# All three branch products of a hybrid mixer by token tile, with the second tile's inputs asked for at that tile

## The chip, the cores and the metric

One core of a Trainium2 chip runs the whole program in one launch. The metric is the device time of one execution in microseconds. Engines: PE multiplies matrices, DVE (vector) and ACT (scalar) work on tiles, POOL does a few small operations, SP issues nearly all transfers. Each engine, and SP's queue too, works through its own instructions in order and waits where one is not ready.

## The reference, cut to what matters

Two layers, each of three blocks on `h` (256 tokens by 1024 channels, float32): a gated feed-forward block, a mixer, a second feed-forward block, each with RMS norms before and after. The mixer projects the normed `h` into the inputs of three branches and three gates:

```python
q, k, v, z, xbc, dt_raw, u, vg, gate_raw = jnp.split(xn @ w_in, split_at, axis=-1)
y_a = moba_attention(q, k, v)                      # 8 heads x 128, causal, ALiBi; 256 tokens are one block
y_s = rms_norm(ssd_scan(...) * jax.nn.silu(z), g)  # state space branch, chunks of 128 tokens
y_c = u * (tril(sgu_w) @ layer_norm(gelu(vg)))     # spatial gating, chunks of 128 tokens
merged = gates[0] * (y_a @ p_attn) + gates[1] * (y_s @ p_ssm) + gates[2] * (y_c @ p_sgu)
return merged @ w_out
```

Tokens lie in two tiles of 128. Attention is causal and the scan runs forward, so the first tile's rows of `y_a` and `y_s` depend on the first tile alone, and the second tile's on both.

## The kernel before, in words

**Matmuls.** Every weight comes as blocks of 128x1024 (512 KB) on SP's queue into a ring of six (`raw`, `load`, L157). `split` (L174) turns a block into two halves, `whi` by a cast on ACT (L180) and `wlo` by a subtraction on DVE (L181), in a ring of `SPLIT` = 11 pairs; splitting a block frees its `raw` buffer and so lets SP issue the next load. `gemm` (L217) walks over (block, token tile): one such **unit** is two products of three matmuls each (L213 to L215: high by high, high by low, low by high; 128x512 each). Activations are held in the same two halves (`xh`, `xl`).

**Order of a gemm.** By default each block is used for tile 0 and then tile 1. The first `head` and the last `tail` blocks go by tile instead: all of them for tile 0, then all of them for tile 1. A block is given back (`done`, L185) at its last unit; only then may another block be split into its place.

**Order of the rest.** All other work is written as generators (`spawn`, L115). After each unit `pump` (L198) advances a counted clock by 1.3 and gives each task its turn when the time that it has yielded has run out; a task's `yield W[...]` is thus a distance counted in units of matmul work. `finish` (L135) runs tasks to their end on the spot. This fixes the order of instructions in each engine's queue; on the chip each engine then runs its queue as the data allow. `pump` also splits at most one waiting block per unit.

**The mixer** (L488, order from L947). Projections `xbc`, `z`, `q`, `k`, `v`; the state space task `ssd` (L678) runs beside `q`, `k` and `v`. For each tile and each group of eight heads it makes decay weights (`ssw`: DVE L709, four exponentials on ACT L713, DVE L715), waits `W["w2"]`, and multiplies (`yd`, L738; for tile 1 also `yo`, L744). At a tile's end it spawns `turned` (L663), which takes `y` through DRAM to turn it (`turn`, L276: a DVE transposition and four DMAs out; `land`, L284: one DMA back) and makes the halves `ysh`, `ysl` (L673 to L675).

`attention` (L781) is one task for both tiles. Per tile: scores (`qk`, L798), bias (L802) and maximum (L807) on DVE, exponentials on ACT (L814), division and `turn` of the probabilities `sc` (L820, L823), `land` (L827), a wait `W["pv"]`, then the products with `v` (`pv`, L837) and their halves `yah`, `yal` (`halves`, L300) in two groups of heads. Tile 1 does not begin before the flag `free` is set, after the first branch.

`branch` (L925) projects one gate (16 units), finishes what its input needs, and multiplies the input with the branch's weights (eight blocks, 16 units, tile `br`); `merge` (L906) multiplies by the gate and adds into `merged`. The first branch is the state space one (with `merged` taken from the ring of 16 large buffers, `b4`), then `vg` is projected, the second is attention's, then `u` is projected, the third is the spatial gating's. The third has `tail=8`, that is, all of its blocks go by tile; the other two have `tail=0`.

Of the kernel before, what the change touches and what calls it, by code (L numbers as in the profile page):

```python
# [12 lines left out]
AF = mybir.ActivationFunctionType  # L13
# [3 lines left out]
P = 128  # L17
# [34 lines left out]
def trunk(ctx, tc, a):  # L52
# [31 lines left out]
    def tr(name):  # L84
        return psum.tile([P, 512], F32, name=name, tag="tr", bufs=TR)

    def small(name, n, dt=F32, bufs=2):
        return sm.tile([P, n], dt, name=name, tag=name, bufs=bufs)
# [161 lines left out]
    def chunk(key, kt=KD, n=512):  # L250
        per = 1024 // n
        return [[(b * per + j, j * n, n, key, b * per + j == 0, b * per + j == kt - 1) for j in range(per)]
                for b in range(kt // per)]
# [22 lines left out]
    def turn(src, m, e=128):  # L276
        V.transpose(src, src)
        rd = dram.tile([m, 4, 32, 4, e], F32, name=f"turn{m}_{e}", tag=f"turn{m}_{e}", bufs=8)
        for b in range(4):
            nc.sync.dma_start(rd[:, :, :, b, :].rearrange("m c i e -> i (m c) e"),  # L280
                              src[32 * b:32 * b + 32].rearrange("p (x e) -> p x e", e=e))
        return rd

    def land(dst, rd):  # L284
        nc.sync.dma_start(dst, rd.rearrange("m c i a e -> (c i) m (a e)"))
# [14 lines left out]
    def halves(ps, hi, lo):  # L300

        p3 = ps.rearrange("p (k t) -> p k t", k=4)
        A.copy(hi, p3)
        V.tensor_tensor(lo, p3, hi.bitcast(F32), op=ALU.subtract)
# [183 lines left out]
    def mixer(l, x, r2, nxt):  # L488
# [189 lines left out]
        def ssd(ysx, rs):  # L678
# [40 lines left out]
            for t in range(NT):  # L719
                for g in range(SG):  # L720
                    weights(t, 2 * g)
                    if t == 0:
                        scaled(g)
                    yield W["w1"]
                    weights(t, 2 * g + 1)
                    if t == 0:

                        pst = tr("state")
                        T.matmul(pst, bc["b"][:, g * P:(g + 1) * P], xw[:, 512 * g:512 * g + 512],
                                 start=True, stop=True)  # L730
                        A.copy(state[:, 512 * g:512 * g + 512], pst)
                    yield W["w2"]
                    c = slice(512 * g, 512 * g + 512)
                    py = tr("yd")
                    for q in (2 * g, 2 * g + 1):
                        for j in range(4):
                            hh = q * 4 + j
                            T.matmul(py[:, (hh - 8 * g) * SP:(hh - 8 * g + 1) * SP], ws[t, q][:, j, :],  # L738
                                     xdt[t][:, hh * SP:(hh + 1) * SP], start=True, stop=True)
                        ws.pop((t, q))  # L740
                    V.tensor_tensor(y[t][:, c], py, y[t][:, c], op=ALU.add)
                    if t == 1:
                        po = tr("yo")
                        T.matmul(po, cT(g, 1), state[:, c], start=True, stop=True)  # L744
                        tmp = b2("yo")
                        V.tensor_tensor(h3(tmp, 8), h3(po, 8),
                                        st["eac"][:, 8 * g:8 * g + 8, None].to_broadcast([P, 8, SP]), op=ALU.mult)
                        V.tensor_tensor(y[t][:, c], y[t][:, c], tmp, op=ALU.add)
                    V.tensor_tensor(y[t][:, c], y[t][:, c], zs[t][:, c], op=ALU.mult)
                rs[t] = rsqrt([sumsq(y[t], "sy")], "rs", 1.0 / D)  # L750
                yt[t] = spawn(turned(t, y[t], pl[:, G_SSM:G_SSM + 8]), wait=1.3 if t else 6.5)
# [26 lines left out]
                A.activation(vv[t][:, 512 * c:512 * c + 512], ps[t], AF.Copy, scale=r2[t])  # L778
            yield W["vv"]

        def attention(yax, free):  # L781
            for t in range(NT):
                while t and not free:
                    yield 0

                m = t + 1
                n = m * P
                per = 512 // n
                sc, s4 = {}, {}
                mx = small("mx", NH)  # L790
                for g in range(2):
                    sc[g] = (b4 if t else b2)("sc", (P, 4 * n))
                    s4[g] = sc[g].rearrange("p (b h j) -> p h b j", h=4, j=32)
                    for u in range(0, 4, per):
                        ps = tr("qk")
                        for j in range(per):
                            hh = u + j
                            T.matmul(ps[:, j * n:(j + 1) * n], qk["q", g][:, hh, t * P:(t + 1) * P],  # L798
                                     qk["k", g][:, hh, 0:n // 32], start=True, stop=True)
                        for j in range(per):  # L800
                            hh = u + j
                            V.scalar_tensor_tensor(s4[g][:, hh], alibi[t].rearrange("p (b j) -> p b j", j=32),  # L802
                                                   2.0 ** -(4 * g + hh + 1),
                                                   ps[:, j * n:(j + 1) * n].rearrange("p (b j) -> p b j", j=32),
                                                   op0=ALU.mult, op1=ALU.add)
                        yield W["qs"]
                    V.tensor_reduce(mx[:, 4 * g:4 * g + 4], s4[g], axis=AX.XY, op=ALU.max)  # L807
                nmx = small("nmx", NH)
                V.tensor_scalar(nmx, mx, -1.0, None, op0=ALU.mult)
                den = small("den", NH)  # L810
                for g in range(2):
                    for j in range(4):
                        c = slice(4 * g + j, 4 * g + j + 1)
                        A.activation(s4[g][:, j], s4[g][:, j], AF.Exp, bias=nmx[:, c], accum_out=den[:, c])  # L814
                    yield W["ex"]
                rden = small("rden", NH)
                V.reciprocal(rden, den)
                rd = {}
                for g in range(2):
                    V.tensor_tensor(sc[g].rearrange("p (b h j) -> p b h j", h=4, j=32),  # L820
                                    sc[g].rearrange("p (b h j) -> p b h j", h=4, j=32),
                                    rden[:, None, 4 * g:4 * g + 4, None].to_broadcast([P, 4 * m, 4, 32]), op=ALU.mult)
                    rd[g] = turn(sc[g], m)  # L823
                    yield 1.3
                yield W["so"]
                for g in range(2):
                    land(sc[g].rearrange("p (m e) -> p m e", m=m), rd[g])  # L827
                yield W["pv"]
                hi, lo = yax.new(t)
                for g in range(2):  # L830

                    pts = sc[g].rearrange("p (m a h j) -> p m h a j", m=m, a=4, h=4)
                    po = tr("pv")
                    for j in range(4):
                        hh = 4 * g + j
                        for k in range(t + 1):
                            T.matmul(po[:, j * P:(j + 1) * P], vv[k][:, hh * HD:(hh + 1) * HD], pts[:, k, j],  # L837
                                     start=k == 0, stop=k == t)
                    halves(po, hi[:, 4 * g:4 * g + 4, :], lo[:, 4 * g:4 * g + 4, :])
                    yield 1.3  # L840


        uu, vg = {}, {}
# [78 lines left out]
                yield W["mg"]  # L922
                yield from to_parts(merged[t], *then.new(t))

        def branch(bx, rs, need, first=False, then=None):  # L925
            store = {}
            es = []
            for c in range(2):
                [ps] = project("gate")
                es.append(spawn(gate_evac(store, c, ps, rs)))  # L930
            finish(*need)
            finish(*es)
            slots, dst = accs("br")
            ready, out = set(), {}

            def on_done(key, t):
                ready.add((key, t))
                if t not in out:
                    out[t] = spawn(merge(t, slots, ready, store, first, then))

            gemm(chunk(0) + chunk(1), bx.h, bx.l, dst, tail=8 if then is not None else 0, on_done=on_done)
            return out

        ysx, yax, ycx, mx = XT("ys"), XT("ya"), XT("yc"), XT("mg")
# [17 lines left out]
        finish(ss)  # L962
        finish(*at)
        free = []
        att = spawn(attention(yax, free))
        b0 = branch(ysx, rs, [ss, *yt.values()], first=True)
        free.append(True)
        gl = []
        for c in range(2):
            gl.append(spawn(gelu_evac(vg, "vg", c, project("vg")[0])))  # L970
        b1 = branch(yax, None, [att, *b0.values()])
        gw = spawn(spatial_weights(l))
        finish(*gl)
        gl = [spawn(gelu_evac(uu, "u", 0, project("u")[0]))]
# [204 lines left out]
```

## Time and profile before

| | us |
|---|---|
| median of three runs | 1488.76 (1488.53 to 1488.9) |
| the profiled execution | 1487.31 |
| its span, first to last instruction | 1485.5 |
| PE busy in it | 1458.3 |
| DVE busy | 970.1 |
| ACT busy | 767.6 |
| mean granted clock of PE | 0.997 of full speed |

Times in the rows are microseconds from the span's start. Layer 0's mixer is used for the stretches; layer 1's runs the same way some 734 us later. In a timeline a row in brackets gives the idle time of that engine just before the instruction and what ended it. The granted clock is a share of full speed: 1.00 is 2.4 GHz, 0.50 is 1.2 GHz.

### The profile page before, as it was taken

How to read it: one execution, taken by the hardware profiler on the slowest of the kernel's cores; microseconds unless marked ns; L12 is line 12 of the kernel's file. 1: busy time of each engine (PE TensorE's matmuls, PEld its weight loads, DVE VectorE, ACT ScalarE, POOL GpSimd, SP SyncE). 2: the span in 40 equal slices, each digit the busy share in tenths (PEclk: the TensorE clock that was granted, in tenths of full speed). 3: DMA queues.
4: the chain of work that ended last, by engine and by line, in shares of the span. 5: the costliest groups of instructions: out<-in, count | busy, mean ns of one | idle time of the engine just before them, and what ended most of it. 6: DMA issues, size and time to landing. Idle time of an engine off the chain costs nothing.

```text
span 1485.5 us, 18564 instructions
## 1 busy us (share of the span) xinstructions
PE 1458.3 (98%) x6706; PEld 1204.4 (81%) x6706; DVE 970.1 (65%) x1188; ACT 767.6 (52%) x1051; POOL 57.0 (4%) x98
## 2 busy tenths in 40 slices
PE   9999999999989999999999999999999899999998
PEld 6888888777878888888888888888778788888886
DVE  6766477777666857666486564876776667676652
ACT  6544367555464537544364443765553644464441
POOL 0000021000000001000000000210000000000000
PEclk9999999999999999999999999999999999999999
DMA  8977655577567445877458874656774765477860
GB/s 291 333 227 255 198 185 183 156 201 246 190 216 228 167 155 197 284 242 255 154 193 281 252 254 128 217 169 172 250 230 155 232 206 170 136 265 245 260 200 28
DMA packets 151003, 312.23 MB, mean 210 GB/s; under 512 B 35456, under 2 KB 76544, under 8 KB 150912
## 3 DMA queue, kind: packets, MB, share of 16 engines
q1 hardware_dynamic: 150336, 310.73, 64.6%
q8 instruction: 52, 0.85, 0.2%
q10 hardware_dynamic: 576, 0.33, 0.1%
q14 instruction: 39, 0.32, 0.1%
HBM read 288.98 MB, written 22.02 MB: 209 GB/s over the span
## 4 chain that ended last, share of the span: by engine, by line
PE 61%; DVE 9%; ACT 3%; DMA 3%; issue 2%; POOL 0%; SPq 0%; DVEq 0%; ACTq 0%; POOLq 0%
PE gu L213 8%; PE gu L215 8%; PE gu L214 8%; DVE wlo L181 5%; PE dn L213 4%; PE dn L215 4%; PE dn L214 4%; PE br L213 3%; PE br L215 3%; PE br L214 3%; ACT whi L180 1%; PE wo L213 1%; PE wo L215 1%; PE u L215 1%; PE u L214 1%
## 5 line engine op out<-in xcount | busy, mean ns | idle before, releaser
L181 DVE TENSOR_TENSOR wlo<-raw,whi 128x1024 fp32r<-128x1024 f32 x495 | 595.3, 1225 | 330.1 <-ACT whi L180 329.5
L180 ACT CAST whi<-raw 128x1024 fp32r<-128x1024 f32 x495 | 512.3, 1051 | 404.5 <-PE gu L215 162.8
L213 PE MATMUL gu<-whi,xh 128*128 128x512 f32 x704 | 276.0, 392 | 1.9 <-ACT xh L328 1.5
L214 PE MATMUL gu<-wlo,xh 128*128 128x512 f32 x704 | 274.9, 390 | 0.0
L215 PE MATMUL gu<-whi,xl 128*128 128x512 f32 x704 | 274.6, 390 | 0.0
L213 PEld LDWEIGHTS gu<-whi,xh 128*128 128x128 f32 x704 | 132.5, 188 | 30.2 <-ACT xh L328 2.0
L215 PEld LDWEIGHTS gu<-whi,xl 128*128 128x128 f32 x704 | 132.5, 188 | 28.2 <-DVE xl L329 0.6
L214 PEld LDWEIGHTS gu<-wlo,xh 128*128 128x128 f32 x704 | 132.5, 188 | 28.2 <-DVE wlo L169 0.9
L213 PE MATMUL dn<-whi,hTh 128*128 128x512 f32 x352 | 137.5, 391 | 0.0
L215 PE MATMUL dn<-whi,hTl 128*128 128x512 f32 x352 | 137.0, 389 | 0.0
L214 PE MATMUL dn<-wlo,hTh 128*128 128x512 f32 x352 | 136.9, 389 | 0.0
L215 PEld LDWEIGHTS dn<-whi,hTl 128*128 128x128 f32 x352 | 66.1, 188 | 13.9
L214 PEld LDWEIGHTS dn<-wlo,hTh 128*128 128x128 f32 x352 | 66.1, 188 | 13.5
L213 PEld LDWEIGHTS dn<-whi,hTh 128*128 128x128 f32 x352 | 66.1, 188 | 13.3
L213 PE MATMUL gate<-whi,xh 128*128 128x512 f32 x192 | 76.6, 399 | 0.0
L215 PE MATMUL gate<-whi,xl 128*128 128x512 f32 x192 | 74.9, 390 | 0.0
L214 PE MATMUL gate<-wlo,xh 128*128 128x512 f32 x192 | 74.8, 389 | 0.0
L328 ACT CAST xh<-xg 128x512 fp32r<-128x512 f32 (+1 forms) x25 | 15.1, 603 | 62.1 <-DVE xg L326 62.1
L713 ACT ACTIVATE ssw<-ssw,nacs 128x128 f32<-128x128 f32 x64 | 20.5, 390 | 49.6 <-DVE ssw L709 49.6
L215 PEld LDWEIGHTS gate<-whi,xl 128*128 128x128 f32 x192 | 36.0, 188 | 7.7
L214 PEld LDWEIGHTS gate<-wlo,xh 128*128 128x128 f32 x192 | 36.1, 188 | 6.9
L417 ACT ACTIVATE silu<-gu,r 128x512 f32<-128x512 f32 (+1 forms) x48 | 31.4, 654 | 19.9 <-PE gu L215 16.2
(239 smaller groups left out, 2229.3 us busy)
## 6 DMA issues: line engine op xcount, KB each, us to landing
raw<-in_mix SPq DMA_DIRECT2D x232, 512.0 KB, 4.4
raw<-in_gu SPq DMA_DIRECT2D x175, 512.0 KB, 4.9
raw<-in_dn SPq DMA_DIRECT2D x88, 512.0 KB, 4.5
turn<-hh SPq DMA_DIRECT2D x160, 64.0 KB, 1.8
hh<-turn SPq DMA_DIRECT2D x40, 256.0 KB, 5.3
row_ffn_post_g<-in_ffn_post_g SPq DMA_DIRECT2D x4, 512.0 KB, 5.2
turnw<-qtok SPq DMA_DIRECT2D x32, 64.0 KB, 2.6
qT<-turnw SPq DMA_DIRECT2D x4, 512.0 KB, 6.1
```

The lines of the kernel that those rows point to most:

```text
L180: A.copy(hi, w)
L181: V.tensor_tensor(lo, w, hi.bitcast(F32), op=ALU.subtract)
L213: T.matmul(o, xh(k, t), hi[:, off:off + n], start=first, stop=False)
L214: T.matmul(o, xh(k, t), lo[:, off:off + n], start=False, stop=False)
L215: T.matmul(o, xl(k, t), hi[:, off:off + n], start=False, stop=last)
L328: A.copy(o_h, xg)
L417: A.activation(silu[t][:, :w], gate(t), AF.Silu, scale=r2[t])
L713: A.activation(w[:, j, :], w[:, j, :], AF.Exp, bias=st["nacs"][:, c:c + 1])
```

## The change

All branch products go by token tile (`tail=8` in every branch). The first two branches no longer finish both tiles' inputs ahead of their gemm: the second tile's input is asked for (`late`, through `guarded` and `gate_on`, which call `finish` at the first use of tile 1) when the order comes to that tile. For that attention becomes one task per tile; the first is finished after the first branch, before `free` is set. Two steps are longer for the second tile: the one ahead of `yd` by 1.3, the one ahead of `pv` by 6.5 of the planner's count.

```diff
@@ ssd
-                    yield W["w2"]
+                    yield W["w2"] + 1.3 * t
@@ attention: the loop over t becomes an argument, its body is moved out by one level and otherwise the same, but for
-        def attention(yax, free):
-            for t in range(NT):
-                while t and not free:
-                    yield 0
+        def attention(t, yax, free):
+            while t and not free:
+                yield 0
...
-                yield W["pv"]
+            yield W["pv"] + 6.5 * t
@@ branch
-        def branch(bx, rs, need, first=False, then=None):
+        def branch(bx, rs, need, late=None, first=False, then=None):
...
-            gemm(chunk(0) + chunk(1), bx.h, bx.l, dst, tail=8 if then is not None else 0, on_done=on_done)
+            if late is not None:
+                bx = guarded(bx, gate_on(late, finish))
+            gemm(chunk(0) + chunk(1), bx.h, bx.l, dst, tail=8, on_done=on_done)
@@ mixer
-        att = spawn(attention(yax, free))
-        b0 = branch(ysx, rs, [ss, *yt.values()], first=True)
+        att = {t: spawn(attention(t, yax, free)) for t in range(NT)}
+        b0 = branch(ysx, rs, [ss], yt, first=True)
+        finish(att[0])
         free.append(True)
...
-        b1 = branch(yax, None, [att, *b0.values()])
+        b1 = branch(yax, None, [*b0.values()], att)
```

## Rows read from the trace of the kernel before

**Rows 1.** The page, its first part: busy time, share of the span and instructions of each engine.

```profile
PE 1458.3 (98%) x6706; PEld 1204.4 (81%) x6706; DVE 970.1 (65%) x1188; ACT 767.6 (52%) x1051; POOL 57.0 (4%) x98
```

**Rows 2.** The waits of PE over the whole span, longest in total first: engine, tile and line, what it waited for, us in total, times, longest.

```profile
PE pv L837 <- DMA sc<-turn: 8.3, 2, 4.2
PE yd L738 <- DVE ssw L715: 4.7, 4, 1.4
PE br L213 <- ACT ysh L674: 3.1, 2, 1.6
...
```

**Rows 3.** The timeline of PE around the second tile's `pv`, layer 0 and then layer 1: start, duration, instruction, count, idle time before it.

```profile
428.28 3.50 PE L837 MATMUL pv<-sc,v 128*128 128x128 f32 x16 [4.09 <-DMA sc<-turn]
431.54 0.48 PE L213 MATMUL gate<-whi,xh 128*128 128x512 f32 x1
...
433.01 1.95 PE L837 MATMUL pv<-sc,v 128*128 128x128 f32 x16
434.71 0.48 PE L213 MATMUL gate<-whi,xh 128*128 128x512 f32 x1
...
1162.30 3.43 PE L837 MATMUL pv<-sc,v 128*128 128x128 f32 x16 [4.16 <-DMA sc<-turn]
```

**Rows 4.** Stretches of the span: from and to, length, busy time of PE, PE's weight loads, DVE, ACT and POOL, then the granted clock of PE, the DMA share and GB/s. The first is the stretch behind the second tile's `pv` wait, the second the one behind the `br` wait.

```profile
428.28:431.50 3.22, 3.22 (x15) 3.22 (x16) 1.82 (x4) 2.46 (x5) 0.00 (x0) 0.52 1.03 388
...
368.00:372.00 4.00, 4.00 (x17) 3.00 (x18) 3.05 (x5) 2.81 (x4) 0.00 (x0) 1.00 0.97 372
```

**Rows 5.** The timeline of PE around `yd`, layer 0: the second group of the first tile, then the two groups of the second tile, each with the instruction that follows it.

```profile
301.04 1.89 PE L738 MATMUL yd<-xs,ssw 128*128 128x64 f32 x16
302.74 0.48 PE L707 MATMUL seg<-acsr,sel 128*128 128x512 f32 x1
...
314.19 1.00 PE L738 MATMUL yd<-xs,ssw 128*128 128x64 f32 x8
...
317.58 1.08 PE L744 MATMUL yo<-state,conv 128*128 128x512 f32 x2
...
330.60 1.00 PE L738 MATMUL yd<-xs,ssw 128*128 128x64 f32 x8
...
333.44 1.08 PE L744 MATMUL yo<-state,conv 128*128 128x512 f32 x2
```

**Rows 6.** The timeline of PE, layer 0: the first tile's first scores; then in the first branch the end of the first unit, the wait for the second tile's halves, the start of the third unit and the first tile's `pv`, behind the fourth unit.

```profile
342.57 1.05 PE L798 MATMUL qk<-kT,qT 128*128 128x128 f32 x8
...
365.95 0.39 PE L215 MATMUL br<-whi,ysl 128*128 128x512 f32 x1
367.88 0.50 PE L213 MATMUL br<-whi,ysh 128*128 128x512 f32 x1 [1.55 <-ACT ysh L674]
...
369.64 0.39 PE L213 MATMUL br<-whi,ysh 128*128 128x512 f32 x1
...
372.37 1.05 PE L837 MATMUL pv<-sc,v 128*128 128x128 f32 x8
```

**Rows 7.** The tile `br`, the instructions that write it: here the second branch's first matmuls, with shortest, median and longest duration in ns, and the first and the last start (layer 0 and layer 1).

```profile
L213 PE MATMUL br<-whi,yah x64: 389/389/389, 447.1 to 1202.1; 128*128 128x512 f32 x64
```

**Rows 8.** The timeline of SP's queue, layer 0: issues of DMAs, merged where one line issues several in a row; the duration of a merged row reaches to the last issue's end. `raw<-in_mix` are weight loads, `turn<-sc` and `sc<-turn` the probabilities' way out and back (first tile, then second), `y<-turn` the second tile's landing of `y`.

```profile
353.80 0.38 SPq L285 DMA_DIRECT2D y<-turn  x1
359.53 0.33 SPq L160 DMA_DIRECT2D raw<-in_mix  x1
361.11 3.73 SPq L280 DMA_DIRECT2D turn<-sc  x8
...
365.91 0.89 SPq L285 DMA_DIRECT2D sc<-turn  x2
...
417.96 5.54 SPq L160 DMA_DIRECT2D raw<-in_mix  x2
423.61 0.93 SPq L285 DMA_DIRECT2D sc<-turn  x2
```

**Rows 9.** DMA issues, KB each and median us from issue to landing: `y<-turn` over the whole span, then `sc<-turn` in the stretch from 364 to 380.

```profile
y<-turn SPq DMA_DIRECT2D x4, 512.0 KB, 5.1
...
sc<-turn SPq DMA_DIRECT2D x2, 256.0 KB, 5.2
```

**Rows 10.** The timeline of DVE, layer 0: the end of the first tile's `ysl` and the first tile's first scores; the second tile's `y` and three splits behind it; `merged` in the first branch; the second tile's first scores.

```profile
349.15 0.69 DVE L675 TENSOR_TENSOR ysl<-y,ysh 128x512 fp32r<-128x512 f32 x1 [0.69 <-ACT ysh L674]
349.76 0.48 DVE L802 SCALAR_TENSOR_TENSOR sc<-con,qk 128x128 f32<-128x128 f32 x2
...
366.49 0.69 DVE L673 TENSOR_TENSOR y<-y,par 128x512 f32<-128x512 f32 x1
...
370.81 3.50 DVE L181 TENSOR_TENSOR wlo<-raw,whi 128x1024 fp32r<-128x1024 f32 x3 [0.27 <-ACT whi L180]
...
389.15 1.29 DVE L916 TENSOR_TENSOR merged<-br,gate 128x512 f32<-128x512 f32 x2 [9.46 <-PE br L214]
...
397.22 0.41 DVE L802 SCALAR_TENSOR_TENSOR sc<-con,qk 128x256 f32<-128x256 f32 x1
```

**Rows 11.** The stretch of the third branch's product, layer 0, columns as in rows 4.

```profile
518.10:541.00 22.90, 22.90 (x108) 18.93 (x107) 14.36 (x18) 10.91 (x14) 0.00 (x0) 1.00 0.44 142
```

**Rows 12.** The line of `pv`, looked at around the first tile's products: the semaphore instructions of PE's weight load queue, with the first and the last time, in layer 0 and in layer 1.

```profile
L837 PEldq EVENT_SEMAPHORE  x2: 51/51/51, 371.0 to 371.9; - x2
...
L837 PEldq EVENT_SEMAPHORE  x2: 51/51/51, 1105.1 to 1105.8; - x2
```

More of the change, by code (lines that the diff above doesn't have):

```diff
@@ L779, in v_evac @@
             yield W["vv"]
-        def attention(yax, free):
-            for t in range(NT):
-                while t and not free:
-                    yield 0
[L786 to L827, printed above, removed]
-                yield W["pv"]
[L829 to L840, printed above, removed]
@@ new lines, in attention @@
+        def attention(t, yax, free):
+            while t and not free:
+                yield 0
+            m = t + 1
+            n = m * P
+            per = 512 // n
+            sc, s4 = {}, {}
+            mx = small("mx", NH)
+            for g in range(2):
+                sc[g] = (b4 if t else b2)("sc", (P, 4 * n))
+                s4[g] = sc[g].rearrange("p (b h j) -> p h b j", h=4, j=32)
+                for u in range(0, 4, per):
+                    ps = tr("qk")
+                    for j in range(per):
+                        hh = u + j
+                        T.matmul(ps[:, j * n:(j + 1) * n], qk["q", g][:, hh, t * P:(t + 1) * P],
+                                 qk["k", g][:, hh, 0:n // 32], start=True, stop=True)
+                    for j in range(per):
+                        hh = u + j
+                        V.scalar_tensor_tensor(s4[g][:, hh], alibi[t].rearrange("p (b j) -> p b j", j=32),
+                                               2.0 ** -(4 * g + hh + 1),
+                                               ps[:, j * n:(j + 1) * n].rearrange("p (b j) -> p b j", j=32),
+                                               op0=ALU.mult, op1=ALU.add)
+                    yield W["qs"]
+                V.tensor_reduce(mx[:, 4 * g:4 * g + 4], s4[g], axis=AX.XY, op=ALU.max)
+            nmx = small("nmx", NH)
+            V.tensor_scalar(nmx, mx, -1.0, None, op0=ALU.mult)
+            den = small("den", NH)
+            for g in range(2):
+                for j in range(4):
+                    c = slice(4 * g + j, 4 * g + j + 1)
+                    A.activation(s4[g][:, j], s4[g][:, j], AF.Exp, bias=nmx[:, c], accum_out=den[:, c])
+                yield W["ex"]
+            rden = small("rden", NH)
+            V.reciprocal(rden, den)
+            rd = {}
+            for g in range(2):
+                V.tensor_tensor(sc[g].rearrange("p (b h j) -> p b h j", h=4, j=32),
+                                sc[g].rearrange("p (b h j) -> p b h j", h=4, j=32),
+                                rden[:, None, 4 * g:4 * g + 4, None].to_broadcast([P, 4 * m, 4, 32]), op=ALU.mult)
+                rd[g] = turn(sc[g], m)
+                yield 1.3
+            yield W["so"]
+            for g in range(2):
+                land(sc[g].rearrange("p (m e) -> p m e", m=m), rd[g])
+            yield W["pv"] + 6.5 * t
+            hi, lo = yax.new(t)
+            for g in range(2):
+                pts = sc[g].rearrange("p (m a h j) -> p m h a j", m=m, a=4, h=4)
+                po = tr("pv")
+                for j in range(4):
+                    hh = 4 * g + j
+                    for k in range(t + 1):
+                        T.matmul(po[:, j * P:(j + 1) * P], vv[k][:, hh * HD:(hh + 1) * HD], pts[:, k, j],
+                                 start=k == 0, stop=k == t)
+                halves(po, hi[:, 4 * g:4 * g + 4, :], lo[:, 4 * g:4 * g + 4, :])
+                yield 1.3
```

## The prediction

> **What bounds the kernel now.** The page comes first: the matrix engine PE is busy for 1458.3 of 1485.5 us [rows 1], so at most some 27 us of its idle time are there to win, plus whatever PE does at a slow clock. Second, the list of whom PE waited for: almost all of that idle time has three causes, each once or twice per layer, and all three lie in the part of the mixer that is changed [rows 2]: the products with `v` (`pv`, 8.3 us in two waits) for the second tile's probabilities to come back from DRAM, the state space products (`yd`, 4.7 us in four) for the vector engine DVE, and the first branch product (`br`, 3.1 us in two) for the second tile's halves. Third, the timeline of PE around each wait, which shows what it costs beyond its idle time, and fourth the granted clock in stretches cut at the waits. PE's work itself does not change, so the gain is what these waits cost now, less what is late next. That is read from the timelines of SP and DVE.
>
> **What each wait costs.** *Second tile's `pv`:* PE idles 4.09 us and then takes from 428.28 to 431.54 for sixteen products that take from 433.01 to 434.71 the next time [rows 3]: 3.26 against 1.70. The granted clock explains it: 0.52 over these 3.2 us, which is the 1.2 GHz level, and 1.00 elsewhere [rows 4]. Cost 4.09 + 1.56 = 5.65 us in layer 0; layer 1 idles 4.16 and then again runs slowly [rows 3], so 11.3 in both. *`yd`:* an undisturbed group of sixteen takes 302.74 - 301.04 = 1.70 us; the second tile's two take 317.58 - 314.19 = 3.39 and 333.44 - 330.60 = 2.84 [rows 5], so 1.69 and 1.14 are lost. *`br`:* after the matmul at 365.95 the next should start at 366.18 (pitch 0.227: twelve matmuls from 369.64 to 372.37) and the seventh at 367.54; it starts at 369.64 [rows 6]. Lost: 2.1 us, with the clock at 1.00 after it [rows 4].
>
> **The change, part by part.** One unit of the order (one tile, one weight block, six matmuls) is 1.36 us of PE, and the planner counts it as 1.3.
>
> *Longer step at the second tile's `pv`* (6.5 more, five units, 6.8 us of PE): PE came to the wait at 428.28 - 4.09 = 424.2 and would now come at about 431.0 less what it gains before; the probabilities were there at 428.2. The wait and the slow stretch go: -5.65 a layer. The step moves `pv`, two casts on ScalarE and two subtractions on DVE, and no DMA; its results are first needed in the second half of the second branch. That branch starts at 447.1 now [rows 7], 12.4 us after the last of these products (434.71), and its second half 10.9 us later still, so nothing pays.
>
> *Longer step in the second tile's state space groups* (one unit each): 1.36 of 1.69 and all of 1.14 go, 2.5 us a layer. Everything behind them in that task moves back two units: a square sum, the POOL steps for `rs`, a DVE transposition, four DMAs to DRAM and the landing of `y`. That landing, issued at 353.80, may fall behind the next weight load, which is issued at 359.53 [rows 8]; with 5.1 us to land [rows 9] `y` is there by 365, and DVE takes it up only at 366.49 [rows 10]. It is then needed in the second half of the branch, after 376 (four units behind the first tile's `pv`, which starts at 371 or later). Cost zero; if that cover went, the old 2.1 us would come back.
>
> *First branch by tile, second tile asked for there:* the first eight units need only the first tile, so the 2.1 us go. `merged` of the first tile takes its slot once the first tile's halves are read, at mid branch instead of near its end; DVE waits there until 389.15 now and so starts the second tile's scores at 397.22 [rows 10]. Behind that wait stand only the second `yal` and splits that have no block to go into before mid branch. Later work on DVE is freed by several us, a second cover for the `pv` landing.
>
> *All eight weight blocks held over the first half* (both branches, both layers): no block is given back for eight units, then one per unit. Eight splits then fall into 10.9 us; on DVE they are 8 x 1.17 = 9.4 us (three take 3.50 [rows 10]). Eleven blocks are split ahead, so the block that is first late is needed seven units and three whole blocks later, 9.5 + 8.2 = 17.7 us. The third branch already runs in this order: 22.9 us with PE busy throughout [rows 11]. I take zero; below zero nothing, as PE has the same matmuls; above, only a lag of over 17.7 us would show. Asking explicitly for the first tile's attention after the first branch costs nothing: its last products stand in that branch's first half already.
>
> *What is late next:* the first tile's `pv`, four units into the first branch. It starts at 372.37 now [rows 6] and is no wait in the list. But PE's queue passes its semaphore only at 371.0, and at 1105.1 in layer 1 [rows 12], and that is the landing: issued at 365.91 [rows 8], 5.2 us to land [rows 9], 371.1. So this product has about 1.1 us to spare, allowing 0.2 from landing to matmul. The chain behind it does not follow PE: DVE goes from the last `ysl` at 349.15 straight to the first scores at 349.76 [rows 10], 7 us after PE began them at 342.6 [rows 6], and then scores, exponentials, transposition, eight DMA issues and the landing follow one another. If PE arrives 2.5 + 2.1 = 4.6 us earlier, it waits 3.5 and keeps 1.1. Bounds: the chain stays put (keep 1.1) or comes earlier with PE (keep 4.6). I take 1.1, since the rows show DVE behind.
>
> *The clock after that new wait:* 4.09 us of idling ended in a half-clock stretch worth 1.56 us, 1.55 us of idling in none [rows 3, 4, 6]. A wait of 3.5 is nearest to the first: I take 1.5 a layer, and keep zero for the range. The Trainium skill speaks against the change here: "TensorE: Matmul & The Clock Gate", section "HAM oscillation", says that an array left waiting for a transfer is throttled again and that every such wait pays for it anew. By that rule the sum below stands, by the 1.55 us row it would be 3 us better; the trace agrees with the page at `pv` (0.52) and shows no drop at `br` (1.00).
>
> **Sum.** Per layer 5.65 + 1.1 - 1.5 = 5.25, for both 10.5 us. The profiled execution took 1487.31 us (its span is 1485.5), so 1476.8; the three runs' median, 1488.76, stands 1.45 above it: **1478.3 us**.
>
> **Rivals.** *No half clock after the new wait:* 2 x 6.75 = 13.5 us, 1475.3. For it: the wait is shorter than any that cost the clock, and shorter still if `yd` gives back less than 2.5. *The first tile's chain comes earlier as well:* all of 5.65 + 2.5 + 2.1 = 10.25 a layer, 1468.3. For it: the longer steps reorder DVE's queue, where short waits could close; against: the amount of DVE work ahead of the scores is the same. *The second tile's `pv` wait remains:* its landing at 423.61 stood behind a weight load that took until 423.5 to be issued [rows 8]. If the bunched splits put it behind a later one by over 6 us, the change does not do what it says: 2 x (1.1 - 1.5) = -0.8, 1489.6; with half of it left about 1484. Against: DVE is freed earlier in that stretch. *Slower:* the same mechanism at the first tile's `pv`. If its landing is queued on SP behind weight loads whose splits are the three from 370.81 to 374.31, themselves behind the second tile's `y` [rows 10], it is issued at 374.4, lands at 379.6 and `pv` starts 7.4 us later than now, plus 1.5 for the clock: 2 x (8.9 - 5.65) = 6.5 us slower, 1495.3. It decides the sign from an issue at 371.3 on, which is behind the first of the three. Against: the steps of `y` move back, the landing does not.
>
> **Chances.** Forecast 0.36, no half clock 0.25, chain earlier 0.20, `pv` wait left 0.13, slower 0.06. The range leaves out the slower case, the `pv` case but for its best part, and the end of the full gain: 1469 to 1482. About 0.2% (3 us) is what a measurement here tells from no change: faster by more 0.86 (the first three and a part of the fourth), within it 0.08, slower 0.06.
>
> **What would show it.** Right: no wait of PE at the second tile's `pv`; no `br` wait for `ysh`; `yd` waits of at most 0.4 us; a new wait of 3 to 4 us at the first tile's `pv` for `sc<-turn`, in each layer, with a granted clock near 0.5 behind it; `merged` on DVE at mid branch; no PE wait for `whi` or `wlo` in or after a branch. Wrong: scores of the first tile clearly earlier against PE's position than now, a landing that waits behind weight loads, or PE waiting for weights at `vg` or `u`.

## The result and the profile after

The changed kernel takes **1474.2 us** (median; 1472.77 to 1474.91) against 1488.64 (1487.57 to 1488.9): a ratio of 0.9903, 95% interval 0.9886 to 0.992. That is 14.4 us, where 10.5 were forecast. The profiled execution took 1472.77 us, its span is 1471.0. PE is busy for 1453.2 us in place of 1458.3 [rows 1]: the same matmuls, without the two stretches at half clock behind `pv`, which were worth some 3 of these 5 us. (Lines behind the changed functions have moved: `pv` is L836 here, scores L801, `merged` L915.)

The waits of PE, to set beside [rows 2]:

```profile
PE seg L707 <- DVE y L741: 3.5, 2, 1.7
PE pv L836 <- DMA sc<-turn: 1.7, 1, 1.7
PE gu L213 <- ACT xh L328: 1.5, 1, 1.5
PE pv L836 <- ACT ysh L674: 1.4, 1, 1.4
PE warm L1024 <- DVE ones L98: 1.0, 1, 1.0
PE sv L881 <- DVE ycl L322: 0.8, 1, 0.8
```

The 8.3, 4.7 and 3.1 us of before are gone from the top. What is there is new: a wait at `pv` once per layer (1.4 and 1.7 us, first tile), and `seg`, which waited 0.9 us in both layers together before and now waits 3.5. The timeline of PE, the second tile's `pv`, answers to [rows 3]:

```profile
428.99 1.95 PE L836 MATMUL pv<-sc,v 128*128 128x128 f32 x16
432.16 1.95 PE L836 MATMUL pv<-sc,v 128*128 128x128 f32 x16
```

No wait, and both groups at full pace. Stretches, with the granted clock third from the end, behind this product and behind the first tile's `pv` in layer 0 and in layer 1 (as [rows 4]):

```profile
428.90:432.10 3.20, 3.20 (x24) 2.94 (x23) 3.20 (x4) 3.20 (x5) 0.00 (x0) 1.00 0.68 215
...
370.40:374.00 3.60, 3.57 (x24) 3.29 (x25) 3.29 (x4) 3.60 (x7) 0.00 (x0) 1.00 0.90 316
...
1096.80:1100.30 3.50, 3.43 (x23) 3.20 (x24) 3.25 (x5) 3.31 (x5) 0.00 (x0) 1.00 0.89 324
```

The timeline of PE at `yd`, second tile (as [rows 5]), with the `seg` between the groups, and then, in the second fence, that same `seg` in the kernel before:

```profile
315.39 2.18 PE L738 MATMUL yd<-xs,ssw 128*128 128x64 f32 x16
317.41 1.08 PE L744 MATMUL yo<-state,conv 128*128 128x512 f32 x2
...
323.21 0.47 PE L707 MATMUL seg<-acsr,sel 128*128 128x512 f32 x1 [1.74 <-DVE y L741]
...
333.06 1.89 PE L738 MATMUL yd<-xs,ssw 128*128 128x64 f32 x16
334.79 1.08 PE L744 MATMUL yo<-state,conv 128*128 128x512 f32 x2
```

```profile
322.10 0.50 PE L707 MATMUL seg<-acsr,sel 128*128 128x512 f32 x1 [0.47 <-DVE y L741]
```

The groups take 2.02 and 1.73 us (3.39 and 2.84 before), but 1.27 us of that come back at `seg`, where PE needs a PSUM buffer that DVE has yet to read (L741). The first tile's `pv` in both layers, on PE and then on SP's queue, to set beside [rows 6] and [rows 8]:

```profile
368.65 0.39 PE L215 MATMUL br<-whi,ysl 128*128 128x512 f32 x1
370.43 1.13 PE L836 MATMUL pv<-sc,v 128*128 128x128 f32 x8 [1.39 <-ACT ysh L674]
...
1096.87 1.13 PE L836 MATMUL pv<-sc,v 128*128 128x128 f32 x8 [1.69 <-DMA sc<-turn]
```

```profile
359.50 0.38 SPq L285 DMA_DIRECT2D y<-turn  x1
...
365.45 0.88 SPq L285 DMA_DIRECT2D sc<-turn  x2
...
420.01 0.93 SPq L285 DMA_DIRECT2D sc<-turn  x2
```

In layer 0 the list names ACT's `ysh` as the releaser, but `pv` does not read it; the first half of the probabilities, issued at 365.45 and 4.8 us under way, landed at 370.3, 0.1 us before the product starts, as layer 1 says of the same wait:

```profile
sc<-turn SPq DMA_DIRECT2D x1, 256.0 KB, 4.8
```

DVE around it, as [rows 10]:

```profile
348.56 0.69 DVE L675 TENSOR_TENSOR ysl<-y,ysh 128x512 fp32r<-128x512 f32 x1 [0.69 <-ACT ysh L674]
349.17 0.88 DVE L801 SCALAR_TENSOR_TENSOR sc<-con,qk 128x128 f32<-128x128 f32 x4
...
377.79 0.69 DVE L915 TENSOR_TENSOR merged<-br,gate 128x512 f32<-128x512 f32 x1 [2.63 <-PE br L214]
...
384.92 4.97 DVE L181 TENSOR_TENSOR wlo<-raw,whi 128x1024 fp32r<-128x1024 f32 x4
...
391.54 0.75 DVE L801 SCALAR_TENSOR_TENSOR sc<-con,qk 128x256 f32<-128x256 f32 x2
```

`merged` comes at mid branch (389.15 before), the splits follow in the second half, and the second tile's scores start at 391.54 in place of 397.22.

**Where the time went, by stage.** First matmul of a stage, in us after the mixer's first matmul, layer 0 / layer 1, worked out from the starts in the profiles, one execution of each kernel (experiments included, for below):

| kernel | first branch | `vg` | second branch | `wo` |
|---|---|---|---|---|
| before | 171.3 / 171.4 | 197.0 / 197.2 | 253.6 / 253.7 | 347.5 / 347.6 |
| changed | 170.2 / 169.9 | 195.5 / 195.4 | 246.2 / 246.2 | 340.1 / 340.7 |
| e1, second `pv` step alone | 171.4 / 171.1 | 197.1 / 196.8 | 247.9 / 247.5 | 341.7 / 341.4 |
| e2, by tile alone | 171.2 / 172.0 | 196.0 / 196.5 | 250.9 / 249.7 | 345.4 / 344.1 |
| e3, state space step alone | 170.2 / 170.3 | 199.5 / 200.2 | 256.1 / 256.7 | 350.0 / 350.6 |
| e4, changed less second `pv` step | 170.0 / 170.0 | 195.2 / 195.3 | 250.1 / 248.7 | 344.8 / 343.5 |
| e5, changed + first `pv` step | 170.3 / 170.0 | 193.9 / 193.6 | 244.6 / 244.4 | 339.0 / 338.9 |
| e6, changed + `seg` step | 167.9 / 168.0 | 197.3 / 198.3 | 248.0 / 249.0 | 342.0 / 343.6 |
| e7, changed + both | 168.0 / 167.9 | 191.6 / 191.5 | 242.3 / 242.2 | 336.5 / 336.8 |
| e8, second branch in default order | 170.1 / 170.4 | 197.4 / 195.5 | 248.1 / 246.2 | 342.0 / 340.1 |
| e9, all steps, not by tile | 168.1 / 168.3 | 201.4 / 200.7 | 252.3 / 251.5 | 346.2 / 345.4 |
| e10, e5 less state space step | 171.3 / 173.8 | 194.9 / 197.4 | 245.6 / 248.1 | 340.3 / 342.0 |

From before to changed, 1.1 and 1.5 us are won ahead of the first branch, 0.4 and 0.3 in it, 5.8 in both layers between `vg` and the second branch, nothing after (0.7 lost in layer 1, at `sv`).

### The profile page after: what moved, and what is told of

Its sections match the earlier page's. It is cut to its first block, busy times and chain, and to the rows that moved or that the text cites. A ratio compares the mean times of both kernels' runs of the same rounds, so it can differ in the third digit from the quotient of the medians.

```text
span 1471.0 us, 18566 instructions
## 1 busy us (share of the span) xinstructions
PE 1453.2 (99%) x6706; PEld 1201.9 (82%) x6706; DVE 971.4 (66%) x1188; ACT 766.9 (52%) x1051; POOL 56.9 (4%) x98
```

## The experiments

Theory: nearly all of it is the second tile's `pv` wait with its half clock. What the order by tile and the state space step win up to the first branch is cut off at the first tile's `pv`, whose data come by a chain that PE does not move. Rivals: the order by tile does the work by freeing DVE; or each wait removed is worth what it cost.

**e1: the second tile's `pv` step alone**, in the kernel before.

```diff
-                yield W["pv"]
+                yield W["pv"] + 6.5 * t
```

> The kernel before with the longer step ahead of the second tile's pv alone. Theory (most of the gain is the second tile's pv wait with its half clock, and the longer step alone removes it): 11.3 us faster than before, no PE wait at the second tile's pv, the br wait of 1.5 us and the yd waits left as they were. Rival (the order by tile is what frees DVE, and the step only follows): under 5 us faster.

Measured: 1475.47 against 1488.87 us, ratio 0.9914 (0.9901 to 0.9928). Its waits of PE:

```profile
PE yd L738 <- DVE ssw L715: 4.6, 4, 1.4
PE br L213 <- ACT ysh L674: 3.1, 2, 1.5
```

The `pv` wait is gone, the other two are as before. By the ratio the gain is 12.8 us (10.7 to 14.7), which holds the 11.3 expected. This one line is most of the change: from `vg` to the second branch it takes 50.7 us in both layers, as the changed kernel does (56.5 before). The rival falls. All else in the change moves the ratio from 0.9914 to 0.9903, less than the intervals tell apart.

**e2: the order by tile alone**, and **e4: the changed kernel without the second `pv` step**; in e2 the state space step is at its old length too.

```diff
-                    yield W["w2"] + 1.3 * t     # e2 only
+                    yield W["w2"]
...
-            yield W["pv"] + 6.5 * t             # e2 and e4
+            yield W["pv"]
```

> The changed kernel with both steps at their old lengths: only the order by tile and the late asking are left. Theory: the br wait goes (2.1 us a layer), of which about 1 is kept because the first tile's pv then waits about 1 us for its landing; and DVE, no longer held at merged until the end of the branch, brings the second tile's probabilities back 3 to 4 us earlier, so that its pv waits 1 to 2 us in place of 4.1 and without a half clock: 8 to 10 us faster than before. Rival (the order by tile removes the br wait and nothing else): 2 to 4 us faster, with the second tile's pv waiting 4 us or more and a half clock behind it.

> The changed kernel with the old step ahead of the second tile's pv, all else as changed. Theory: PE comes to that product 6.8 us earlier than in the changed kernel, at about 422.2 in layer 0, and the probabilities land at about 424.6, so it waits about 2.4 us: 5 us slower than the changed kernel without a half clock behind it, 8 with one. Rival (the order by tile alone covers the landing): within 1 us of the changed kernel.

Measured: e2 1481.29 us, ratio 0.9949 (0.9936 to 0.9961), 7.6 us faster than before; e4 1482.25, 0.996 (0.9947 to 0.9972), some 8 us slower than the changed kernel. PE in e2, first tile's `pv`, then second tile's in both layers; the stretch behind the second; then the second tile's in e4:

```profile
371.03 1.13 PE L836 MATMUL pv<-sc,v 128*128 128x128 f32 x8 [0.96 <-DMA sc<-turn]
...
425.32 3.58 PE L836 MATMUL pv<-sc,v 128*128 128x128 f32 x16 [2.38 <-DMA sc<-turn]
...
1157.31 2.02 PE L836 MATMUL pv<-sc,v 128*128 128x128 f32 x16 [2.17 <-DMA sc<-turn]
```

```profile
425.30:428.60 3.30, 3.28 (x15) 3.30 (x16) 1.90 (x4) 2.54 (x5) 0.00 (x0) 0.50 1.04 410
```

```profile
424.34 3.65 PE L836 MATMUL pv<-sc,v 128*128 128x128 f32 x16 [2.34 <-DMA sc<-turn]
...
1155.62 2.02 PE L836 MATMUL pv<-sc,v 128*128 128x128 f32 x16 [2.44 <-DMA sc<-turn]
```

So the order by tile does shorten this wait, from 4.1 to between 2.2 and 2.4 us, and cannot remove it. It does so by DVE being free earlier: in e2's layer 0 DVE takes up the first tile's `merged` at 378.38 and the second tile's scores at 392.13 (389.15 and 397.22 before), and the landing is issued 2.8 us earlier, counted from the mixer's first matmul. In layer 0 a half clock followed (0.50), in layer 1 none (sixteen products in 2.02 us). e2's theory had the wait and its price too small: 1 to 2 us, and no half clock. Its layer 1 also lost time ahead of the first branch, to a half clock behind a `yd` wait (last section). The rivals of both runs fall: the order by tile does more than the `br` wait, and less than cover the landing. The two runs differ by the state space step alone, and it gains nothing here (1481.29 without, 1482.25 with it).

**e3: the state space step alone**, in the kernel before.

```diff
-                    yield W["w2"]
+                    yield W["w2"] + 1.3 * t
```

> The kernel before with the longer state space step of the second tile alone. Theory (what comes earlier here is taken back at the next thing that does not follow PE): the yd waits go but the seg wait grows to 1.7 us and the br wait for the second tile's halves grows by about as much as is left, so within 1.5 us of the kernel before. Rival (the yd waits are worth what they cost): 2.5 to 5 us faster.

Measured: 1492.84 us, ratio 1.0027 (1.0016 to 1.0037): slower. Both expectations miss. Its waits, and the stretch behind the `br` wait:

```profile
PE pv L837 <- DMA sc<-turn: 8.0, 2, 4.0
PE br L213 <- ACT ysh L674: 7.0, 2, 3.5
PE seg L707 <- DVE y L741: 3.5, 2, 1.7
```

```profile
368.60:372.00 3.40, 3.35 (x9) 2.36 (x10) 2.43 (x4) 2.04 (x3) 0.00 (x0) 0.66 1.02 386
```

PE is at the first branch 1.1 us earlier and there waits 3.5 us for the second tile's halves in place of 1.5, since the step moves `y` back: its landing is issued at 359.66 in place of 353.80. Behind this wait there is a half clock (0.66; 0.50 in layer 1), which the theory had left out. In these runs the step pays only where the second tile is asked for late and the first tile's `pv` no longer waits: e2 and e4 show that the first alone is not enough, e10 below has both.

**e5, e6, e7: the two new waits taken away**, one by one and together, in the changed kernel.

```diff
-            yield W["pv"] + 6.5 * t
+            yield W["pv"] + (6.5 if t else 2.6)             # e5; 3.9 in e7
...
-                    yield W["w1"]
+                    yield W["w1"] + (1.3 if t and g else 0)   # e6, e7
```

> The changed kernel with the step ahead of the first tile's pv longer as well, by 2.6 (two units, 2.7 us of PE). Theory (the first tile's probabilities land at a time that PE does not set, and the changed kernel's waits of 1.4 and 1.7 us there are what is left of the order by tile's gain): no PE wait at either pv, 3 us faster than the changed kernel, near 1471. Rival (the wait only moves: the second half of the first branch or the second tile's pv takes it over): within 1 us of the changed kernel.

> The changed kernel with one unit more between the two score products (seg) of the second tile's second group, where PE waits 1.74 us a layer for DVE. Theory: that wait goes, PE comes to the first tile's pv 1.3 to 1.7 us earlier, the landing there stays where it is, and the wait there grows from 1.4 to 1.7 us to about 3: no gain, 0 to 3 us slower if a half clock follows. Rival (each wait is worth what it costs): 2.5 to 3.5 us faster than the changed kernel.

> The changed kernel with both: one unit more between the second tile's last two seg products, and the first tile's pv step longer by 3.9 (three units, since PE comes there earlier). Theory: the two waits go together, 3 us from the first tile's pv and 2.5 to 3.5 from seg, 5.5 to 6.5 us faster than the changed kernel, near 1468. Rival (as for the first alone, seg is not worth its time): 3 us faster, no more than the step at the first pv alone.

Measured, against 1487.49 us of the kernel before in the same runs: e5 1469.41, ratio 0.9878 (0.9864 to 0.9891); e6 1477.06, 0.993 (0.9917 to 0.9942); e7 **1465.15**, 0.985 (0.9836 to 0.9863). The first tile's `pv` in e6, layer 0, and the stretches behind it in layer 0 and layer 1; then the longest waits of e7:

```profile
370.39 2.04 PE L836 MATMUL pv<-sc,v 128*128 128x128 f32 x8 [3.96 <-DMA sc<-turn]
```

```profile
370.20:373.50 3.30, 3.10 (x11) 2.87 (x12) 2.36 (x4) 2.48 (x4) 0.00 (x0) 0.51 1.03 413
...
1098.80:1102.10 3.30, 3.30 (x12) 3.01 (x13) 2.36 (x4) 2.54 (x4) 0.00 (x0) 0.50 1.00 400
```

```profile
PE sv L881 <- DVE ycl L322: 1.1, 2, 0.7
PE warm L1024 <- DVE ones L98: 1.0, 1, 1.0
PE gu L213 <- ACT xh L328: 1.0, 1, 1.0
```

This is the theory in its plainest form. e5 has no wait at either `pv` and is 3.1 us faster than the changed kernel in the profiled executions, as expected (4.8 by the medians). Taking away the `seg` wait alone makes the kernel 3 to 4 us slower than the changed one: PE is at the first branch 2 us earlier, waits 3.96 us at the first tile's `pv` (3.89 in layer 1), and pays a half clock in both layers. The same step is worth 4.3 us (e5 to e7) once that product has been moved back far enough, by one unit more in e7. e7 beats the changed kernel by some 8 us, 1.5 to 2 more than expected: ahead of the first branch it wins 2.2 and 2.0 us, where 1.25 to 1.75 a layer were expected. Why that is more stays open.

**e8: the second branch in the default order**, both attention tiles finished ahead of it.

```diff
-        def branch(bx, rs, need, late=None, first=False, then=None):
+        def branch(bx, rs, need, late=None, first=False, then=None, tail=8):
...
-            gemm(chunk(0) + chunk(1), bx.h, bx.l, dst, tail=8, on_done=on_done)
+            gemm(chunk(0) + chunk(1), bx.h, bx.l, dst, tail=tail, on_done=on_done)
...
-        b1 = branch(yax, None, [*b0.values()], att)
+        b1 = branch(yax, None, [*att.values(), *b0.values()], tail=0)
```

> The changed kernel with the second branch (attention's) back in the default order, both tiles' attention finished ahead of it. Theory (attention's second tile is done well before this branch begins, so its order by tile neither gains nor costs): within 1 us of the changed kernel. Rival (it matters that the second tile is asked for late): 2 us slower or more, with a PE wait at br for yah. Other rival (holding eight blocks costs something): 1 us faster or more.

Measured: 1473.96 us, ratio 0.9907 (0.9893 to 0.992), the same as changed. The branch itself takes 21.8 us either way, and both rivals fall. What differs in its profiled execution is layer 0's first `pv`, where a wait of 1.92 us was followed by this stretch, while 1.25 us in layer 1 were not (1.00):

```profile
371.40:374.80 3.40, 3.40 (x15) 2.82 (x14) 3.40 (x5) 2.48 (x4) 0.00 (x0) 0.58 0.78 277
```

**e9: all four steps without the order by tile**, and **e10: e5 with the state space step at its old length.**

```diff
-                yield W["pv"]                             # e9, in the kernel before
+                yield W["pv"] + (6.5 if t else 3.9)
...
-                    yield W["w2"]
+                    yield W["w2"] + 1.3 * t
...
-                    yield W["w1"]
+                    yield W["w1"] + (1.3 if t and g else 0)
```

```diff
-            yield W["pv"] + 6.5 * t                       # e10, in the changed kernel
+            yield W["pv"] + (6.5 if t else 2.6)
...
-                    yield W["w2"] + 1.3 * t
+                    yield W["w2"]
```

> The kernel before with all four longer steps (state space group 1.3, between the last seg products 1.3, first tile's pv 3.9, second tile's pv 6.5), but without the order by tile and the late asking. Theory (with nothing late at the pv products, the order by tile is worth the whole wait for the second tile's halves): PE comes to the first branch 3.3 us earlier than in the kernel before while the halves come 1 us later, so it waits 5 to 6 us at br for ysh, with a half clock behind it: 12 to 16 us slower than the same steps with the order by tile (1465), so 1477 to 1481. Rival (the order by tile is worth the 2.1 us a layer that the wait costs before): 1469 to 1470.

> The order by tile with the longer steps at both pv (2.6 and 6.5), the state space step at its old length. Theory (the state space step is worth what PE gains up to the first branch, 1.1 us a layer, once the first tile's pv no longer waits): 2 us slower than with it (1469.4), near 1471.5, with the yd waits of 1.4 and 0.9 us back. Rival (its yd waits are worth 2.8 us a layer): 1475.

Measured: e9 1483.79 us, ratio 0.9975 (0.9966 to 0.9983); e10 1472.43, 0.9896 (0.9881 to 0.9911); the kernel before 1487.62. PE and DVE in e9 at the first branch:

```profile
369.89 0.80 PE L213 MATMUL br<-whi,ysh 128*128 128x512 f32 x1 [6.82 <-ACT ysh L674]
```

```profile
368.50 0.69 DVE L673 TENSOR_TENSOR y<-y,par 128x512 f32<-128x512 f32 x1 [1.14 <-DMA y<-turn]
```

PE waits 6.8 us for the second tile's halves (7.1 in layer 1), more than expected, as `y` now also lands late. So the order by tile is worth nearly 19 us beside e7's steps (12 to 16 expected), while beside e1's step it was worth about one, the state space step included. e10 shows the state space step worth some 2 to 3 us, near the theory's 2. Part of that is the half clock that its profiled execution has behind a `yd` wait of layer 1 (last section): that execution is the longest of its four runs (1474.36), and the shortest (1470.82) is 1.4 us above e5.

## Why the prediction was right

- **What bounds the kernel: right, but read too widely.** The three waits are 16.1 of the 27.2 us in which PE does not work, not almost all of them; 6.4 us lie behind PE's last matmul. Nothing in the sum rests on it.
- **Second tile's `pv`, 5.65 us a layer: right.** 5.8 measured in both layers, and e1 has it alone.
- **`yd`, 2.5 us a layer: the term was too large.** 1.1 and 1.5 came through to the first branch. I had left `seg` out, which waited 0.47 us already (its row stands above) behind the same DVE queue and now waits 1.74. The term should have been 2.5 - 1.27 = 1.2. By itself this hardly changes the sum, as what is won ahead of the first tile's `pv` is taken back there; but it makes the wait there shorter.
- **`br` by tile: right.** No wait for `ysh`. That `y` would be issued behind the next weight load and cost nothing was right too (359.50); e3 shows what it costs without the late asking.
- **What is late next: right in place and cause, too large in size.** The wait at the first tile's `pv` is there, 1.4 and 1.7 us where 3.5 stood, since PE came less early by the `seg` wait and the probabilities landed 0.4 and 0.7 us earlier (layer 0 and layer 1). That PE's coming earlier does not bring the landing forward is shown by its issue, counted from the mixer's first matmul in layer 0: 172.4 (before), 172.2 (changed), 172.5, 172.3, 172.2 and 172.0 (e1 to e4), while PE comes to the branch between 170.0 and 171.4. Where the steps reorder DVE's queue further (e6, e7) the issue is at 171.4, 0.8 earlier against PE's 2.2, but the landing takes longer: in all twelve profiles layer 0's first half lands between 176.8 and 178.0. The chain does get later with PE: in layer 1 of e2 and e10, where PE came to the branch at 172.0 and 173.8, the issue was at 173.0 and 174.8.
- **Half clock behind it, 1.5 us a layer: the step that failed.** In the profiled execution the clock stayed at 1.00. This is 3.0 of the 4 us between forecast and result, the rest being mostly what was kept at that product (1.5 and 1.8 us where 1.1 stood). The wait was shorter than the 4.09 us that I classed it with, and it was shorter because of the `seg` wait: e6, which takes that wait away, is the kernel that the forecast had in mind. There PE waits 3.96 and 3.89 us, the clock is at 0.51 and 0.50 behind it, and the gain is 10.4 us, where 10.5 were forecast. The Trainium skill's rule ("TensorE: Matmul & The Clock Gate", section "HAM oscillation") that each such wait is paid for anew held in e3 and e6 at 3.5 to 4.0 us; at 1.4 to 1.7 us the changed kernel's profile does not show it. The other three runs of the changed kernel took 1.2 to 2.1 us longer at a mean granted clock of 0.997 to 0.998, against 0.999 in the profiled one, so some half clock is likely in them too; where it fell is not on record.
- **Holding eight blocks, zero: right.** No PE wait for `whi` or `wlo`; e8 finds no difference.
- **Rivals.** "No half clock" (1475.3) is what the profiled execution shows, by a shorter wait. "Chain earlier" shows in no run by more than 0.9 us: that is the most by which the landing, counted so, comes ahead of that of the kernel before. Nothing of the slower case was seen; its issue of 371.3, from which the sign would turn, leaves out the 0.2 us allowed elsewhere and should be 371.1.

## What to carry to other kernels

A wait removed is worth only the distance to the next thing that does not move with the engine, so look for products that are just in time, with a semaphore passed 1 us ahead of use (as [rows 12] show), before pricing the removal. Price the waits in one stretch together: the same step cost 4 us, or won 4, depending on whether the next one had been moved. Where a tile's input is late, asking for it in the second half of the product covers it (e9 against e7: nearly 19 us), but this shows only once no other wait stands ahead of that half.

## What was not expected of the hardware

Short waits of PE do not have one price. (Half clock is the 1.2 GHz level; a share between 0.5 and 1 is the mean of a stretch with both levels in it.) Of PE's waits for data in the twelve profiles, all ten of 3.5 us and more had a half clock behind them. Among those of 1.2 to 2.5 us some had and some had not: 1.39 and 1.69 not (changed), 2.17 and 2.44 not but 2.38 and 2.34 so (e2, e4), 1.92 so (e8, 0.58). In layer 1 of e2 and e10 it was even so for the 1.41 and 1.44 us ahead of a `yd` product; the stretches are, for e2, the first row here, and for e10 the third:

```profile
1049.80:1053.20 3.40, 3.40 (x10) 2.62 (x9) 3.40 (x4) 1.32 (x2) 0.00 (x0) 0.50 0.85 257
...
1040.00:1044.00 4.00, 2.56 (x17) 2.31 (x15) 2.41 (x4) 2.97 (x6) 0.00 (x0) 0.90 0.63 129
1044.00:1048.00 4.00, 4.00 (x11) 2.68 (x11) 4.00 (x5) 2.39 (x4) 0.00 (x0) 0.50 0.82 243
```

The same `yd` wait had none behind it in layer 0 of both runs, nor in either layer of the kernel before (1.45 and 1.43 us). What decides it stays open.
